# A streaming encoder step: an earlier hand-over of SBUF space at the end of the input projection, and an output projection whose first two tiles run row tile by row tile

## The chip, the cores and the metric

The kernel runs on one core of a Trainium2 chip. The metric is the device time of one execution in microseconds (us). Matmuls run on TensorE (PE); DVE is VectorE, ACT is ScalarE, POOL is GpSimd, and SP is the engine whose queue issues nearly all transfers between HBM and SBUF. "Weight tile" below means 128 output columns of a weight matrix, "row tile" 128 rows of the branch results, all tokens wide.

## The reference, cut to what matters

One layer of an encoder reads 1024 new tokens and 32 tokens of a running stream, 1056 in all, each 1024 wide:

```python
x = layer_norm(x, ln_in_g, ln_in_b)
proj = x @ w_in                                # 17 424 columns
y_a, y_b, y_c, y_d = ...                       # four mixers on columns of proj, each times silu(z)
yb = einsum('blnw,nwd->blnd', ys, w_branch)    # ys stacks the four
gates = sigmoid(col(OFF_G, 4 * D_MODEL) + b_gate)
mixed = einsum('blnd,blnd->bld', gates, yb)
out = mixed @ w_out
x = layer_norm(ALPHA * x + out, ln_g, ln_b)
```

## The kernel before, in words

Activations are kept transposed: 128 channels on the partitions, 1056 tokens along the free axis. For near-float32 accuracy every operand is split into a high part (ACT casts it to fp32r) and a low part (DVE subtracts), and a product is three matmuls: high by high, high by low, low by high. The weight side's split is `wsplit` (L174), the row tiles' is `put_y` (L1323).

The work comes in five stages: the input's normalisation; a first part of the input projection with the mixers A, C and D; the *pairs* (L1012 to L1142); the branch weights (L1343 to L1362); the output projection (L1378 to L1400). The last three are touched.

**Pairs.** The rest of the input projection runs two weight tiles at a time by a fast scheme with seven products in place of eight (L1104 to L1110). It needs sums of halves of the tokens, `TH` and `TL`, for products 2, 3 and 5 (keys 1, 2, 4). They lie in the pool `tt` (L963); the weights' sums and products 5 to 7's operands lie in `w2` (L961). After each product of the last pair `ending(j)` (L1301) runs. After product 5 it closes `tt`, opens the pool `stp` in its place, and starts `stage_y` of the first branch with five row tiles loaded ahead; after product 6 it steps on until two are multiplied.

**Branch weights.** For each branch in the order 0, 3, 2, 1, `stage_y` (L1269) loads for each of eight row tiles a mixer result `t` and its `silu(z)`, both from HBM scratch, and multiplies them (branch 2 has a normalisation and a silu more). `put_y` makes `Y_H` and `Y_L` of them, in the pool `yp`, which takes the place of the input once the pairs are done. Eight jobs, one per weight tile, then multiply them with `w_branch`; each job's eviction multiplies by the gate tile `G` and adds the partial sum `m` of the branches before, which lies in a `padc` tile. The first two jobs run `together` (L230): for each row tile, all three token chunks of both weight tiles, on six PSUM banks. While a branch runs, the next one's row tiles are staged (queue "norm"), and in the last branch `w_out` is loaded and split (L1331).

**Mixing.** The eight `b_mix` generators (L1145) compute mixer B beside all this. The queue "mix" runs them a step at a time, 0.55 steps per turn; a turn comes every few matmuls (`bg`, L169), a step ends at a `yield`. Rate 0 holds the queue during the last pair, and what is left is emptied at once ahead of the third branch (`qm.drain()`, L1371). Convolution tiles and `m` share the two `padc` tiles; `accc` is one tile.

**Output projection.** For token tile 8 (the running stream), then 0 to 7, and for each half of the columns: 24 matmuls over eight row tiles and the three products into one bank, then the residual (L1392) and the layer normalisation. The row tiles are the last branch's `G`.

The tile framework orders each engine's instructions ahead of time by a model of readiness, with the program's order as the priority, and puts in all waits. An instruction that is ready in that model can stand far ahead of its place in the code.

Of the kernel before, what the change touches and what calls it, by code (L numbers as in the profile page):

```python
# [10 lines left out]
F32R = mybir.dt.float32r  # L11
# [42 lines left out]
def encoder_step(ctx: ExitStack, tc: tile.TileContext, I, O):  # L54
# [75 lines left out]
    def ev():  # L130
        return evp.tile([128, T], F32, name="ev")
# [831 lines left out]
    tt = ttc.enter_context(tc.tile_pool(name="tt", bufs=1, side="right"))  # L963
    TH = {j: tt.tile([128, 4, HT], F32R, name=f"th{j}") for j in (1, 2, 4)}
    TL = {j: tt.tile([128, 4, HT], F32R, name=f"tl{j}") for j in (1, 2, 4)}
    lo_t, up_t = slice(0, HT), slice(HT, T)
# [178 lines left out]
    def b_mix(i):  # L1145
# [19 lines left out]
        dve.tensor_sub(xlo, xc, xhi.bitcast(F32))  # L1165
        yield
        g = wk.tile([128, T], F32, name="padc", bufs=2)
        gx = wk.tile([128, T], F32, name="accc", bufs=1)
# [89 lines left out]
    wb = {n: [wb_job(n, d, n != branches[0], n == branches[-1]) for d in range(8)] for n in branches}  # L1258
    stp, first_y = [], []

    def st(dtype=F32, n=T):
        return stp[0].tile([128, n], dtype, name="st", tag="st", bufs=12)

    def sl(dtype=F32, n=T):
        return yp.tile([128, n], dtype, name="sl", tag="sl", bufs=4)

    staged = []

    def stage_y(n, ahead=1):  # L1269

        tz = []

        def load():
            k = len(tz)
            if k < 8:
                tz.append((st(), st()))
                sp.dma_start(tz[k][0], d_t[n][k])
                sp.dma_start(tz[k][1], d_z[n][k])
        if n == 2:
            mu, rs = sl(), sl()  # L1280
            for i, t in enumerate((mu, rs)):
                src = d_mr[9 * i:9 * i + 1, 0:1]
                sp.dma_start(t, bass.AP(tensor=src.tensor, offset=src.offset, ap=[[0, 128], [1, T]]))
        for _ in range(ahead):
            load()
        yield
        yield
        for k, (t, z) in enumerate(tz):
            if n == 2:
                dve.tensor_sub(t, t, mu)  # L1290
                yield
                dve.tensor_mul(t, t, rs)
                act.activation(t, t, AF.Silu, scale=col("c_g", k), bias=col("c_bb", k))
                yield
            dve.tensor_mul(t, t, z)
            load()
            staged.append(t)
            yield
            yield

    def ending(j):  # L1301

        if j == 1:
            qm.rate = 0.0
        if j in (2, 4):
            wb[branches[0]][j // 2 - 1].load()
        if j == 5:
            ttc.close()
            stp.append(ctx.enter_context(tc.tile_pool(name="stp", bufs=1, side="right")))
            first_y.append(stage_y(branches[0], 5))  # L1310
            next(first_y[0])
            next(first_y[0])
        if j == 6:
            while len(staged) < 2:
                next(first_y[0])

# [5 lines left out]

    def put_y(i, y):  # L1323
        Y_H[i] = yp.tile([128, T], F32R, name=f"yh{i}")
        Y_L[i] = yp.tile([128, T], F32R, name=f"yl{i}")
        act.copy(Y_H[i], y)
        dve.tensor_sub(Y_L[i], y, Y_H[i].bitcast(F32))  # L1327

    woh, wol = [], []

    def w_out():  # L1331
        for k in range(KT):
            w = wk.tile([128, T], F32, name="padc", bufs=2)
            o = st if k < 6 else sl
            sp.dma_start(w[:, :D], I["w_out"][k * 128:(k + 1) * 128, :])
            yield
            woh.append(o(F32R, D))
            wol.append(o(F32R, D))
            act.copy(woh[k], w[:, :D])
            dve.tensor_sub(wol[k], w[:, :D], woh[k].bitcast(F32))  # L1340
            yield

    qn = queue("norm", 1.5)  # L1343
    for b, n in enumerate(branches):
        for k in range(8):
            while not staged:
                next(first_y[0])
            put_y(k, staged.pop(0))
        nxt = branches[b + 1] if b + 1 < 4 else None
# [24 lines left out]
    for t, n, i in ((gi, "ln_in", 0), (bi, "ln_in", 1), (go, "ln_out", 0), (bo, "ln_out", 1)):  # L1374
        src = I[n][i:i + 1]
        sp.dma_start(t, bass.AP(tensor=src.tensor, offset=src.offset, ap=[[0, 128], [1, D]]))

    for t in (8, 0, 1, 2, 3, 4, 5, 6, 7):  # L1378
        r = slice(0, 128) if t < 8 else slice(96, 128)
        ts = slice(t * 128, t * 128 + 128) if t < 8 else slice(928, 1056)  # L1380
        xr = wk.tile([128, T], F32, name="padc", bufs=2)[r, :D]
        sp.dma_start(xr, d_x[t, :r.stop - r.start])
        pool.tensor_tensor(xr, xr, gi[r], op=OP.mult)
        pool.tensor_tensor(xr, xr, bi[r], op=OP.add)
        y = ev()
        for c in range(2):
            ps = mmt()
            hs = slice(c * 512, (c + 1) * 512)
            todo = [(a, w, k) for k in range(KT) for a, w in ((Y_H, woh), (Y_L, woh), (Y_H, wol))]
            for n, (a, w, k) in enumerate(todo):  # L1390
                pe.matmul(ps, lhsT=a[k][:, ts], rhs=w[k][:, hs], start=(n == 0), stop=(n == len(todo) - 1))  # L1391
            dve.scalar_tensor_tensor(y[r, hs], xr[:, hs], ALPHA, ps[r], op0=OP.mult, op1=OP.add)  # L1392
# [73 lines left out]
```

## Time and profile before

| | us |
|---|---|
| median of 3 runs | 2256.55 |
| the runs | 2254.4 to 2257.28 |
| the profiled execution | 2259.44 |
| its span, first to last instruction | 2257.7 |
| last pair's last matmul starts | 1747.90 |
| first matmul of the branch weights | 1753.90 |
| first matmul of the output projection | 2144.45 |
| its last matmul starts | 2248.93 |

All positions are counted from the span's start. In the profile, a group or a timeline row names the engine, the line of the code, the operation, and out<-in by the program's tile names: `st<-d_t` is a row tile's load, `yh` and `yl` are Y_H and Y_L, `mm` is a PSUM bank, `accc` and `padc` work tiles. A row of the timeline is: start, duration, then in brackets the idle time before it and what ended that. A row of the waits view is: who waited, for whom, total, number of times, longest. The chain is the work that ended last, followed back step by step.

### The profile page before, as it was taken

What the parts mean: (1) busy time and instruction counts of PE and PEld (TensorE: products, weight loads), DVE (VectorE), ACT (ScalarE), POOL (GpSimd) and SP (SyncE); (2) the same over time, 40 slices, a digit from 0 to 9 for tenths busy, and PEclk for the clock granted to TensorE, in tenths of its full rate; (3) what the DMA queues carried; (4) which work ended last, traced back from release to release, by engine and by line L of the source; (5) the groups of instructions that cost most, each with busy time, mean ns of one, the idle gap of its engine ahead of it and who ended that gap; (6) DMA issues with size and microseconds to landing.
All of it is one profiled execution on the core that took longest, in us unless ns stands there. A gap on an engine that the chain in (4) does not pass through costs nothing.

```text
span 2257.7 us, 38700 instructions
## 1 busy us (share of the span) xinstructions
PE 2198.2 (97%) x15334; PEld 2139.7 (95%) x15334; DVE 1645.8 (73%) x2668; ACT 1006.8 (45%) x1939; POOL 162.0 (7%) x257
## 2 busy tenths in 40 slices
PE   7999999999999999999999999999999999999998
PEld 7999989999999998999999999999999899999976
DVE  7586665599998634778969697966676679855565
ACT  4587876411133443333444444446666245522200
POOL 3121011100000000000000000000000000100043
PEclk9999999999999999999999999999999999999999
DMA  6154454421155564223333333333344898775422
GB/s 233 44 141 126 125 132 108 127 67 48 58 173 177 178 181 135 61 91 99 126 115 114 108 122 127 102 106 121 104 145 137 339 317 309 286 275 173 132 96 75
DMA packets 198160, 323.71 MB, mean 143 GB/s; under 512 B 52793, under 2 KB 117131, under 8 KB 197659
## 3 DMA queue, kind: packets, MB, share of 16 engines
q1 hardware_dynamic: 197979, 321.25, 44.2%
q8 instruction: 120, 1.97, 0.4%
q14 instruction: 61, 0.50, 0.1%
HBM read 211.12 MB, written 110.06 MB: 142 GB/s over the span
## 4 chain that ended last, share of the span: by engine, by line
PE 70%; DVE 9%; DMA 3%; issue 2%; ACT 1%; SPq 0%; DVEq 0%; ACTq 0%
PE mm L1066 31%; PE mm L212 26%; PE mm L1391 4%; PE mm L224 2%; DVE accc L315 2%; DVE bt L564 1%; PE aux L1173 1%; DVE bx L565 1%; DMA Gb<-d_gc 1%; PE aux L679 1%; PE aux L686 1%; DVE yl L1327 1%; PE aux L699 1%; PE aux L698 1%; PE aux L670 1%
## 5 line engine op out<-in xcount | busy, mean ns | idle before, releaser
L315 DVE SCALAR_TENSOR_TENSOR accc<-padc,cols,accc 128x1086 f32<-128x1086 f32 (+2 forms) x250 | 335.1, 1341 | 10.8 <-ACT accc L312 9.4
L212 PE MATMUL mm<-xh,wh 128*128 128x352 f32 (+2 forms) x1600 | 299.4, 325 | 2.7 <-ACT xh L876 0.9
L212 PE MATMUL mm<-xl,wh 128*128 128x352 f32 (+2 forms) x1600 | 301.2, 325 | 0.0
L212 PE MATMUL mm<-xh,wl 128*128 128x352 f32 (+2 forms) x1568 | 295.0, 327 | 3.6 <-DVE wl L181 3.6
L212 PEld LDWEIGHTS mm<-xh,wh 128*128 128x128 f32 x1600 | 259.2, 190 | 5.0 <-DVE padc L737 1.3
L212 PEld LDWEIGHTS mm<-xh,wl 128*128 128x128 f32 x1568 | 257.9, 192 | 5.4 <-DVE wl L181 3.9
L212 PEld LDWEIGHTS mm<-xl,wh 128*128 128x128 f32 x1600 | 259.1, 190 | 1.9 <-issue 0.4
L1066 PE MATMUL mm<-xh,o 128*128 128x264 f32 x1152 | 217.1, 284 | 0.0
L179 ACT CAST wh<-wr 128x1024 fp32r<-128x1024 f32 x96 | 100.7, 1049 | 254.9 <-PE mm L212 212.2
L1066 PEld LDWEIGHTS mm<-xh,o 128*128 128x128 f32 x1152 | 181.3, 188 | 0.0
L1066 PE MATMUL mm<-xl,o 128*128 128x264 f32 x576 | 163.7, 284 | 0.0
L1078 ACT COPY mu<-mm 128x264 f32<-128x264 f32 x216 | 81.0, 377 | 148.2 <-PE mm L1066 146.3
L181 DVE TENSOR_TENSOR wl<-wr,wh 128x1024 fp32r<-128x1024 f32 x96 | 116.8, 1217 | 36.2 <-ACT wh L179 14.7
L1084 DVE TENSOR_TENSOR ev<-mm,mu 128x264 f32<-128x264 f32 x216 | 91.2, 426 | 30.9 <-ACT mu L1078 16.0
L1066 PE MATMUL mm<-xh,wh 128*128 128x264 f32 x576 | 112.3, 285 | 1.1 <-ACT xh L1124 1.1
L1030 ACT CAST o<-wr 128x512 fp32r<-128x512 f32 x108 | 66.8, 619 | 102.4 <-PE mm L1066 86.5
L1066 PE MATMUL mm<-th,o 128*128 128x264 f32 x576 | 112.0, 285 | 0.2
L1066 PE MATMUL mm<-th,wh 128*128 128x264 f32 x576 | 111.8, 285 | 0.0
L1066 PE MATMUL mm<-th,wl 128*128 128x264 f32 x576 | 111.2, 284 | 0.0
L1066 PE MATMUL mm<-xh,wl 128*128 128x264 f32 x576 | 110.6, 284 | 0.0
L1066 PEld LDWEIGHTS mm<-xl,o 128*128 128x128 f32 x576 | 108.2, 188 | 0.0
L212 PE MATMUL mm<-yh,wh 128*128 128x352 f32 x552 | 100.8, 324 | 0.0
(335 smaller groups left out, 4864.9 us busy)
## 6 DMA issues: line engine op xcount, KB each, us to landing
wr<-in_w_in SPq DMA_DIRECT2D x137, 512.0 KB, 3.7
d_z<-ev SPq DMA_DIRECT2D x64, 264.0 KB, 2.2
d_gate<-ev SPq DMA_DIRECT2D x64, 264.0 KB, 2.1
st<-d_t SPq DMA_DIRECT2D x32, 528.0 KB, 6.2
st<-d_z SPq DMA_DIRECT2D x32, 528.0 KB, 8.0
wr<-in_w_branch SPq DMA_DIRECT2D x32, 512.0 KB, 4.4
ev<-d_gate SPq DMA_DIRECT2D x30, 528.0 KB, 5.7
d_mix<-ev SPq DMA_DIRECT2D x24, 528.0 KB, 4.7
```

The source lines that it names most:

```text
L179: act.copy(hi, raw)
L181: dve.tensor_sub(lo, raw, hi.bitcast(F32))
L212: pe.matmul(ps[:, :c[1]], lhsT=w[:, k, :], rhs=r(k)[:, cs(c)], start=(n == 0), stop=(n == len(todo) - 1))
L224: pe.matmul(ps[:, :c[1]], lhsT=w[:, k, :], rhs=r(k)[:, cs(c)], start=(n == 0), stop=(n == len(todo) - 1))
L315: dve.scalar_tensor_tensor(acc, pad[:, i:i + W], col(name, ci, i), acc, op0=OP.mult, op1=OP.add)
L564: dve.tensor_tensor(tv, a[:, j + 1:, j:j + 1].to_broadcast([P, n, m]), x[:, j:j + 1, 0:m].to_broadcast([P, n, m]), op=OP.mult)
L565: dve.tensor_tensor(x[:, j + 1:, 0:m], x[:, j + 1:, 0:m], tv, op=OP.subtract)
L1030: act.copy(t[:, 0:4], src)
L1066: pe.matmul(b, lhsT=w[:, wo + k, :], rhs=XS[name](p, k)[:, sl], start=(start and n == 0), stop=(stop and n == 11), skip_group_check=True)
L1078: act.copy(mu[name][:, c * HC:(c + 1) * HC], b)
L1084: dve.tensor_add(res[i][:, a:a + HC], b, mu[name][:, c * HC:(c + 1) * HC])
L1391: pe.matmul(ps, lhsT=a[k][:, ts], rhs=w[k][:, hs], start=(n == 0), stop=(n == len(todo) - 1))
```

## The change

1. The token sum with key 4 moves from `tt` to `w2`, so `tt` holds two sums and is closed after product 3. `stp` takes its place with 8 tiles in place of 12, and four row tiles of the first branch (`t` and `z`) are loaded at once; two are multiplied after product 5, two after product 6.
2. Row tiles five to eight go into a second set of 8 tiles, `sl` in `yp`, loaded as the first four are put. Their multiplications stand between a tile's cast and its subtraction, one tile ahead.
3. `stage_y` becomes a plain loop, `t` in `st`, `z` in `sl`; `w_out`'s high parts go to `st`, its low parts to `sl`.
4. `b_mix` gets one more `yield` between the split of its convolution and the gate matmuls.
5. The output projection's tiles 8 and 0 run together: for each row tile, three matmuls for each of the four (tile, half) banks. The other seven tiles are as before.

```diff
@@ -961,8 +961,8 @@
     w2 = w2c.enter_context(tc.tile_pool(name="w2", bufs=1))
     ttc = ExitStack()
     tt = ttc.enter_context(tc.tile_pool(name="tt", bufs=1, side="right"))
-    TH = {j: tt.tile([128, 4, HT], F32R, name=f"th{j}") for j in (1, 2, 4)}
-    TL = {j: tt.tile([128, 4, HT], F32R, name=f"tl{j}") for j in (1, 2, 4)}
+    TH = {j: (w2 if j == 4 else tt).tile([128, 4, HT], F32R, name=f"th{j}") for j in (1, 2, 4)}
+    TL = {j: (w2 if j == 4 else tt).tile([128, 4, HT], F32R, name=f"tl{j}") for j in (1, 2, 4)}
     lo_t, up_t = slice(0, HT), slice(HT, T)
 
     def build_t():
@@ -1164,6 +1164,7 @@
         act.copy(xhi, xc)
         dve.tensor_sub(xlo, xc, xhi.bitcast(F32))
         yield
+        yield
         g = wk.tile([128, T], F32, name="padc", bufs=2)
         gx = wk.tile([128, T], F32, name="accc", bufs=1)
         for c in chunks:
@@ -1256,36 +1257,27 @@
 
     branches = (0, 3, 2, 1)
     wb = {n: [wb_job(n, d, n != branches[0], n == branches[-1]) for d in range(8)] for n in branches}
-    stp, first_y = [], []
+    stp = []
 
     def st(dtype=F32, n=T):
-        return stp[0].tile([128, n], dtype, name="st", tag="st", bufs=12)
+        return stp[0].tile([128, n], dtype, name="st", tag="st", bufs=8)
 
     def sl(dtype=F32, n=T):
-        return yp.tile([128, n], dtype, name="sl", tag="sl", bufs=4)
-
-    staged = []
-
-    def stage_y(n, ahead=1):
-
-        tz = []
-
-        def load():
-            k = len(tz)
-            if k < 8:
-                tz.append((st(), st()))
-                sp.dma_start(tz[k][0], d_t[n][k])
-                sp.dma_start(tz[k][1], d_z[n][k])
+        return yp.tile([128, n], dtype, name="sl", tag="sl", bufs=8)
+
+    def stage_y(n, order=None):
+
         if n == 2:
             mu, rs = sl(), sl()
             for i, t in enumerate((mu, rs)):
                 src = d_mr[9 * i:9 * i + 1, 0:1]
                 sp.dma_start(t, bass.AP(tensor=src.tensor, offset=src.offset, ap=[[0, 128], [1, T]]))
-        for _ in range(ahead):
-            load()
-        yield
-        yield
-        for k, (t, z) in enumerate(tz):
+        for k in range(8):
+            t, z = st(), sl()
+            sp.dma_start(t, d_t[n][k])
+            sp.dma_start(z, d_z[n][k])
+            yield
+            yield
             if n == 2:
                 dve.tensor_sub(t, t, mu)
                 yield
@@ -1293,10 +1285,18 @@
                 act.activation(t, t, AF.Silu, scale=col("c_g", k), bias=col("c_bb", k))
                 yield
             dve.tensor_mul(t, t, z)
-            load()
             staged.append(t)
-            yield
-            yield
+
+    staged, first_y = [], []
+
+    def load_first(k, new):
+        first_y.append((new(), new()))
+        sp.dma_start(first_y[k][0], d_t[branches[0]][k])
+        sp.dma_start(first_y[k][1], d_z[branches[0]][k])
+
+    def mul_first(k):
+        t, z = first_y[k]
+        dve.tensor_mul(t, t, z)
 
     def ending(j):
 
@@ -1304,15 +1304,14 @@
             qm.rate = 0.0
         if j in (2, 4):
             wb[branches[0]][j // 2 - 1].load()
-        if j == 5:
+        if j == 3:
             ttc.close()
             stp.append(ctx.enter_context(tc.tile_pool(name="stp", bufs=1, side="right")))
-            first_y.append(stage_y(branches[0], 5))
-            next(first_y[0])
-            next(first_y[0])
-        if j == 6:
-            while len(staged) < 2:
-                next(first_y[0])
+            for k in range(4):
+                load_first(k, st)
+        if j in (5, 6):
+            mul_first(2 * j - 10)
+            mul_first(2 * j - 9)
 
     run_pairs(pairs, ending)
     xstack.close()
@@ -1320,10 +1319,14 @@
     yp = ctx.enter_context(tc.tile_pool(name="yp", bufs=1))
     g2 = yp
 
-    def put_y(i, y):
+    def put_y(i, y, low=True):
         Y_H[i] = yp.tile([128, T], F32R, name=f"yh{i}")
         Y_L[i] = yp.tile([128, T], F32R, name=f"yl{i}")
         act.copy(Y_H[i], y)
+        if low:
+            put_low(i, y)
+
+    def put_low(i, y):
         dve.tensor_sub(Y_L[i], y, Y_H[i].bitcast(F32))
 
     woh, wol = [], []
@@ -1331,11 +1334,10 @@
     def w_out():
         for k in range(KT):
             w = wk.tile([128, T], F32, name="padc", bufs=2)
-            o = st if k < 6 else sl
             sp.dma_start(w[:, :D], I["w_out"][k * 128:(k + 1) * 128, :])
             yield
-            woh.append(o(F32R, D))
-            wol.append(o(F32R, D))
+            woh.append(st(F32R, D))
+            wol.append(sl(F32R, D))
             act.copy(woh[k], w[:, :D])
             dve.tensor_sub(wol[k], w[:, :D], woh[k].bitcast(F32))
             yield
@@ -1343,9 +1345,16 @@
     qn = queue("norm", 1.5)
     for b, n in enumerate(branches):
         for k in range(8):
-            while not staged:
-                next(first_y[0])
-            put_y(k, staged.pop(0))
+            if b == 0:
+
+                if k < 4:
+                    load_first(k + 4, sl)
+                put_y(k, first_y[k][0], False)
+                if 4 <= k + 1 < 8:
+                    mul_first(k + 1)
+                put_low(k, first_y[k][0])
+            else:
+                put_y(k, staged.pop(0))
         nxt = branches[b + 1] if b + 1 < 4 else None
         if nxt == 1:
             qm.drain()
@@ -1375,20 +1384,37 @@
         src = I[n][i:i + 1]
         sp.dma_start(t, bass.AP(tensor=src.tensor, offset=src.offset, ap=[[0, 128], [1, D]]))
 
+    def slices(t):
+        return (slice(0, 128) if t < 8 else slice(96, 128)), (slice(t * 128, t * 128 + 128) if t < 8 else slice(928, 1056))
+
+    def project(ts_):
+
+        pss = {(t, c): mmt() for t in ts_ for c in range(2)}
+        todo = [(a, w, k) for k in range(KT) for a, w in ((Y_H, woh), (Y_L, woh), (Y_H, wol))]
+        for k in range(0, len(todo), 3):
+            for t, c in pss:
+                for n, (a, w, kk) in enumerate(todo[k:k + 3], k):
+                    pe.matmul(pss[t, c], lhsT=a[kk][:, slices(t)[1]], rhs=w[kk][:, c * 512:(c + 1) * 512], start=(n == 0), stop=(n == len(todo) - 1))
+        return pss
+
     for t in (8, 0, 1, 2, 3, 4, 5, 6, 7):
-        r = slice(0, 128) if t < 8 else slice(96, 128)
-        ts = slice(t * 128, t * 128 + 128) if t < 8 else slice(928, 1056)
+        r, ts = slices(t)
         xr = wk.tile([128, T], F32, name="padc", bufs=2)[r, :D]
         sp.dma_start(xr, d_x[t, :r.stop - r.start])
         pool.tensor_tensor(xr, xr, gi[r], op=OP.mult)
         pool.tensor_tensor(xr, xr, bi[r], op=OP.add)
         y = ev()
+        if t == 8:
+            first_ps = project((8, 0))
         for c in range(2):
-            ps = mmt()
             hs = slice(c * 512, (c + 1) * 512)
-            todo = [(a, w, k) for k in range(KT) for a, w in ((Y_H, woh), (Y_L, woh), (Y_H, wol))]
-            for n, (a, w, k) in enumerate(todo):
-                pe.matmul(ps, lhsT=a[k][:, ts], rhs=w[k][:, hs], start=(n == 0), stop=(n == len(todo) - 1))
+            if t in (8, 0):
+                ps = first_ps[t, c]
+            else:
+                ps = mmt()
+                todo = [(a, w, k) for k in range(KT) for a, w in ((Y_H, woh), (Y_L, woh), (Y_H, wol))]
+                for n, (a, w, k) in enumerate(todo):
+                    pe.matmul(ps, lhsT=a[k][:, ts], rhs=w[k][:, hs], start=(n == 0), stop=(n == len(todo) - 1))
             dve.scalar_tensor_tensor(y[r, hs], xr[:, hs], ALPHA, ps[r], op0=OP.mult, op1=OP.add)
         mu, rs = layer_stats(wk, y, r)
         out = O["y_prompt"][ts, :] if t < 8 else O["y_sample"]
```

## The prediction

> **What bounds the kernel now.** First the page: the span, and how full each engine is.
>
> ```profile
> span 2257.7 us, 38700 instructions
> PE 2198.2 (97%) x15334; PEld 2139.7 (95%) x15334; DVE 1645.8 (73%) x2668; ACT 1006.8 (45%) x1939; POOL 162.0 (7%) x257
> ```
>
> TensorE is busy for 97% of the span, so work moved on other engines gives time back only where PE waits or runs at a lowered clock. I read PE's rows of the waits view next, over the three stretches that the diff touches: the pairs' end, the branch weights, the output projection.
>
> ```profile
> PE mm L240 <- ACT yh L1326: 5.7, 1, 5.7
> PE aux L1173 <- ACT ev L1164: 2.5, 2, 2.3
> PE mm L1391 <- ACT yh L1326: 3.1, 1, 3.1
> ```
>
> Each stretch has one long wait: 5.7, 2.3 and 3.1 us. What a wait costs beyond its length is in the windows view (busy time of PE, PEld, DVE, ACT, POOL; granted clock; DMA share; GB/s), here mostly cut where the granted clock changes.
>
> ```profile
> 399.30:402.70 3.40, 1.79 (x12) 1.50 (x11) 0.96 (x2) 3.34 (x11) 0.63 (x1) 1.00 0.84 231
> 402.70:406.10 3.40, 2.45 (x15) 2.17 (x16) 0.90 (x2) 3.11 (x19) 0.00 (x0) 1.00 0.27 77
> 1736.00:1740.00 4.00, 4.00 (x34) 3.80 (x33) 2.11 (x2) 3.67 (x5) 0.00 (x0) 1.00 0.47 145
> 1740.00:1744.00 4.00, 4.00 (x35) 4.00 (x34) 4.00 (x5) 3.33 (x6) 0.00 (x0) 1.00 0.27 68
> 1747.50:1750.90 3.40, 0.68 (x6) 0.47 (x4) 2.03 (x4) 1.47 (x2) 0.00 (x0) 1.00 1.02 409
> 1750.90:1754.30 3.40, 0.40 (x1) 0.40 (x2) 1.68 (x2) 1.07 (x1) 0.00 (x0) 0.51 1.02 414
> 1754.30:1757.70 3.40, 3.40 (x12) 3.19 (x12) 2.26 (x3) 1.07 (x1) 0.00 (x0) 0.50 1.02 413
> 1842.70:1866.00 23.30, 23.30 (x146) 23.30 (x145) 22.05 (x22) 14.40 (x14) 0.00 (x0) 1.00 0.94 319
> 1918.20:1921.60 3.40, 1.12 (x8) 0.82 (x7) 3.40 (x5) 1.07 (x1) 0.00 (x0) 1.00 0.93 332
> 1921.60:1925.00 3.40, 3.40 (x13) 3.40 (x13) 3.32 (x5) 1.28 (x2) 0.00 (x0) 0.50 0.90 292
> 2153.70:2157.10 3.40, 3.40 (x10) 2.61 (x9) 1.47 (x3) 0.00 (x0) 2.00 (x1) 0.50 0.17 70
> ```
>
> The clock is granted in steps of 3.4 us. A step with 1.12 us of PE work is followed by one at 0.50; a step with 1.79 us of work is not. So an idle time of over about 2 us within a step costs another 1.7 us in the next.
>
> **The pairs' end.** The rows, from the timeline, the chain and SP's issues:
>
> ```profile
> 1735.98 0.28 PE L1066 MATMUL mm<-th,wl 128*128 128x264 f32 x1
> 1743.92 0.42 SPq L1277 DMA_DIRECT2D st<-d_t  x1
> 1744.38 6.93 DMA st<-d_z
> 1747.90 0.28 PE L1066 MATMUL mm<-xh,o 128*128 128x264 f32 x1
> 1751.41 1.26 DVE L1295 TENSOR_TENSOR st<-st 128x1056 f32<-128x1056 f32 x1 [1.88 <-DMA st<-d_z]
> 1752.78 1.07 ACT L1326 CAST yh<-st 128x1056 fp32r<-128x1056 f32 x1 [2.48 <-DVE st L1295]
> 1753.88 1.26 DVE L1327 TENSOR_TENSOR yl<-st,yh 128x1056 fp32r<-128x1056 f32 x1 [1.21 <-ACT yh L1326]
> 1755.06 1.25 DVE L1295 TENSOR_TENSOR st<-st 128x1056 f32<-128x1056 f32 x1
> 1782.38 19.12 PE mm L212 x120
> 1808.29 34.48 PE mm L212 x216
> DMA to landing us min/median/max: 6.9/10.1/11.3
> st<-d_t SPq DMA_DIRECT2D x32, 528.0 KB, 6.2
> ```
>
> Now the first row tile is loaded at 1743.92, lands at 1751.3, and is multiplied, cast and subtracted before PE starts. Then each tile passes DVE, ACT, DVE in turn: 3.65 us from one multiplication to the next. PE needs less: 34.48 us for 216 matmuls is 0.1596 us each, so 18 per row tile are 2.87 us. From PE's last matmul of the pairs (1747.90 + 0.12 = 1748.0) to the end of the two weight tiles (1782.4) are 34.4 us, of which 144 x 0.1596 = 23.0 are work.
>
> In the new order the pool is free after the third product, 1735.98 + 0.12 = 1736.1. Eight loads at about 0.45 us of SP each are issued by 1740. They move 8 x 0.54 = 4.3 MB, 10.6 us at 409 GB/s, into a stretch where DMA is at a share of 0.47 and 0.27. They land between 1740 + 6.9 = 1746.9 and 1740 + 11.3 = 1751.3 at the latest; I take 1748, since the queue is empty when they start. SP's later instructions (a weight load and two gate writes) move back by 3.6 us; that weight tile is used at 1782, so it costs nothing. The four multiplications add 4 x 1.26 = 5.0 us to DVE before 1750. DVE has 1.9 us free from 1736 to 1744 and 1.4 from 1747.5 to 1750.9; the rest must displace mixing steps or run up to 1.7 us late. Behind them on DVE wait the last two products' evictions, for whose banks only the second half of a row tile's matmuls waits. PE's twelve Y_H matmuls (1.9 us) cover that.
>
> So after 1748.0: the cast, 1.07 and 0.1 of signalling, PE from 1749.2, then 23.0 us without a gap: 24.2 instead of 34.4, a gain of 10.2. The remaining wait of 1.2 us is below the 1.6 (3.40 - 1.79) that left the clock alone. Row tiles five to eight are loaded from 1748.0 on: at the median landing of 10.1 us the fifth is there at 1758.5 and multiplied at 1759.7, and the fourth tile's subtraction, queued behind it on DVE, ends at 1761.0, against 1749.2 + 3 x 2.87 + 1.9 = 1759.7 when PE wants it: 1.3 late; at 6.9 nothing is late. I take 0.8, nearer to the median. The eighth has until 1769. Forecast: **-9.4**, bounds -10.2 and -4.9 (the second rival).
>
> **The projection.**
>
> ```profile
> 2144.45 0.39 PE L1391 MATMUL mm<-st,yh 128*128 128x512 f32 x1
> 2146.59 0.51 DVE L1248 TENSOR_TENSOR accc<-mm,accc 128x352 f32<-128x352 f32 x1
> 2152.79 0.50 PE L1391 MATMUL mm<-sl,yh 128*128 128x512 f32 x1 [3.08 <-ACT yh L1326]
> 2237.85 0.39 PE L1391 MATMUL mm<-sl,yh 128*128 128x512 f32 x1
> 2243.39 0.39 PE L1391 MATMUL mm<-sl,yh 128*128 128x512 f32 x1
> 2248.93 0.40 PE L1391 MATMUL mm<-sl,yh 128*128 128x512 f32 x1
> ```
>
> Undisturbed, 24 matmuls take 5.54 us, 0.231 each; 431 steps would be 99.5, and 2144.45 to 2248.93 is 104.5. The 5.0 us are the wait for the eighth row tile and the half-clock step after it. New: seven row tiles give 7 x 12 = 84 matmuls, 19.4 us, so the eighth is wanted at 2163.9; it was there at 2152.8. The added wait: four banks at once, where the fourth is freed by the eviction that ends at 2147.1, and PE wants it nine matmuls in, at 2146.5: 0.6 us. The evictions of both first tiles come some 11 us later, beside PE's third tile; the last tile's chain moves with PE. Forecast **-4.4**, bounds -5.0 and -3.1 (the wait alone, the clock falling all the same).
>
> The Trainium skill ("TensorE: Matmul & The Clock Gate", section "Why this matters for your kernels") puts the clock's fall at idle gaps of over some 3 us. The step at 1918.2 with 2.3 us idle contradicts it, and by the rule the first rival would give 1.7 us less.
>
> **The branch weights.** The extra step puts 8 steps more into a queue that advances 0.55 per turn. Rows of the last two mixes:
>
> ```profile
> 1920.18 1.07 ACT L1164 CAST ev<-ev 128x1056 fp32r<-128x1056 f32 x1 [5.12 <-DVE ev L318]
> 1945.64 2.28 DVE L1193 TENSOR_TENSOR_SCAN padc<-accc,ev 128x1024 f32<-128x1024 f32 x1
> 1958.39 0.42 SPq L1148 DMA_DIRECT2D padc<-d_bx  x1
> 1989.86 2.29 DVE L1193 TENSOR_TENSOR_SCAN padc<-accc,ev 128x1024 f32<-128x1024 f32 x1
> ```
>
> The stall at 1918 follows a cast that runs as soon as the convolution (L318) is done, so data set it, not turns. I take **0**: bounds -4.0 (2.3 + 1.7, all of it goes) and +4.0 (a second one like it).
>
> **Without cost.** One token sum in another pool: same bytes, read by the fifth product as before. Staging's z in tiles of their own, w_out split by pool: the same loads and casts; what hides them is PE's queue of matmuls, full at clock 1.00 from 1842.7 to 1866 with DMA at 0.94. Without that cover a late row tile would cost about the 3.65 us of its passage.
>
> **The sum.** 9.4 + 4.4 + 0 = 13.8 us. The profiled execution took 2259.44, 1.7 beyond its span, and would take 2245.6; the median is 2.9 lower: 2256.55 - 13.8 = **2242.8**.
>
> **Rivals.**
> - *The stall at 1918 goes as well*: 4.0 more, 2238.8. For it: the extra step stands exactly between the cast and the matmuls that waited. Against: the reason above.
> - *The early loads come late*: landing 11.3 us after the last issue, the fourth multiplication ends at 1752.6 and the first subtraction, behind it on DVE, at 1753.9, where PE wants it at 1751.1: 2.8 us and 1.7 of clock, 2247.3. For it: those landings stand in the rows. Against: they were measured with DMA full.
> - *The drained mixes hold both padc tiles* (slower). The queue is emptied ahead of the third branch, and by the step count the seventh mix is now almost whole in it. If the third branch's partial sums get no padc tile until both mixes are over, that is 27.7 (1920.18 to 1947.9) + 33.8 (1958.39 to 1992.2) = 61.5 us; the gate tiles last for about four weight tiles, 4 x 72 x 0.1596 = 46.0. PE stalls for 15.5, with three half-clock steps 20.6: 2263.4. It decides once the stall passes 13.8. Against: padc goes to whoever is ready first when one is released.
> - *Changing banks costs clock.* As a mechanism here: every second clock step of the 96 matmuls (22.2 us) at 0.50 makes them 29.6, so 2250.2. Against: the branch weights' bank-by-bank matmuls ran at 1.00 from 1842.7 to 1866. The Trainium skill describes it ("TensorE: Matmul & The Clock Gate", section "A second HAM failure mode: psum-queue depth-cycling"); this case's trace shows no such fall.
> - *The early loads do not start earlier*, the tile framework waiting for more than the two sums: only the projection gains, 2252.2.
>
> **Chances.** Forecast 0.51, stall gone 0.20, late loads 0.13, drained mixes 0.09 (0.05 at full price, 0.04 with one weight tile's 11.5 us, within 0.2%), no earlier start 0.05, clock 0.02. About 0.2%, 4.5 us, is what a measurement of this kernel can tell from no change. Faster: 0.51 + 0.20 + 0.13 + 0.02 = 0.86; same 0.05 + 0.04 = 0.09; slower 0.05. The range runs from all three bounds (10.2 + 5.0 + 4.0, 2237.3) to the clock rival (2250.2).
>
> **What would show it.** Right: eight st loads from about 1736, PE's wait before the first weight tiles near 1.2 us, no half-clock step there, these two tiles in some 25 us; in the projection no wait over 1 us and clock 1.00. Wrong: a multiplication waiting on DMA after 1749, PE waiting on yl, a wait of several us on padc or L1173 between 1860 and 2000 that the old trace has not.

## The result, and the profile after

The changed kernel takes 2268.12 us (median of five runs, 2263.44 to 2272.3) against 2256.06 beside it: 12 us slower, ratio 1.0053 with a 95% interval of 1.0037 to 1.007. The forecast was 2242.8. The profiled execution took 2272.3 us, the slowest of the five.

The page's span and engines, then all of PE's waits from 1000 us on:

```profile
span 2270.6 us, 38698 instructions
PE 2198.8 (97%) x15334; PEld 2142.6 (94%) x15334; DVE 1655.1 (73%) x2668; ACT 1005.6 (44%) x1939; POOL 169.3 (7%) x257
```

```profile
PE aux L1174 <- ACT ev L1164: 7.4, 2, 5.9
PE mm L240 <- DVE yl L1330: 3.5, 1, 3.5
PE mm L1066 <- ACT mu L1078: 2.9, 4, 1.3
PE mm L240 <- ACT yh L1325: 2.5, 1, 2.5
PE aux L1174 <- DVE ev L1165: 2.1, 2, 1.2
PE aux L1174 <- ACT padc L1175: 1.5, 1, 1.5
PE mm L1397 <- DVE accc L1249: 0.4, 1, 0.4
```

PE did the same work (2198.8 us against 2198.2), and the projection's long wait is gone. But PE now waits 11.0 us in all on the mixes' gate matmuls (L1174; L1173 in the code before), 5.9 of it at once, and 3.5 us on a Y_L tile (`yl`) at the pairs' end. The prediction had named both, a new wait of several us on the gates and PE waiting on `yl`, as signs of being wrong. The timeline of ACT, then of PE, at the longest wait (the first row of PE is where the seventh mix's gate matmuls have just ended):

```profile
1983.20 1.28 ACT L312 ACTIVATE accc<-padc,cols 128x1059 f32<-128x1059 f32 x1 [3.87 <-DVE padc L1196]
1989.71 1.07 ACT L1164 CAST ev<-ev 128x1056 fp32r<-128x1056 f32 x1 [4.31 <-DVE ev L318]
```

```profile
1961.60 0.65 PE L224 MATMUL mm<-yh,wh 128*128 128x352 f32 x3
1990.84 0.95 PE L1174 MATMUL aux<-ev,gwh 128*128 128x352 f32 x2 [5.93 <-ACT ev L1164]
```

And the clock around it (windows view, columns as in the prediction), with the one other step at half clock in the branch weights first and that whole stage last:

```profile
1942.09:1945.50 3.41, 3.41 (x14) 3.41 (x13) 1.01 (x3) 2.28 (x3) 0.00 (x0) 0.50 1.02 410
1986.39:1989.81 3.42, 0.00 (x0) 0.00 (x0) 3.26 (x4) 0.10 (x1) 0.00 (x0) 1.00 0.54 165
1989.81:1993.22 3.41, 1.19 (x3) 0.74 (x4) 2.49 (x3) 0.98 (x1) 0.00 (x0) 0.51 1.04 423
1993.22:1996.63 3.41, 1.94 (x6) 1.48 (x7) 3.15 (x7) 2.28 (x3) 0.00 (x0) 0.50 0.89 360
1996.63:2000.05 3.42, 3.42 (x14) 3.42 (x13) 0.00 (x0) 1.53 (x3) 0.00 (x0) 0.50 0.00 0
1786.92:2161.00 374.08, 363.20 (x2235) 361.20 (x2234) 254.92 (x316) 135.89 (x138) 21.22 (x21) 0.98 0.71 248
```

The queue "mix" is emptied ahead of the third branch, so the last mix's gate matmuls stand in PE's queue at a fixed place among the third branch's first matmuls: behind 144 of them, two weight tiles, counted in the trace. PE starts these at 1961.60 and is through at 1990.84 - 5.93 = 1984.9. But the last mix's convolution starts only at 1983.20, when the seventh mix's scan (L1196) has let go of its tiles, and its cast comes at 1989.71. PE stands still, and the next three clock steps run at half.

The last row closes the account of the stage. PE is idle for 374.08 - 363.20 = 10.9 us. In the four steps at half clock it is busy for 3.41 + 1.19 + 1.94 + 3.42 = 10.0 us, which costs half of that, 5.0. The other 358.2 us are work, and by the same working all the kernels below have 357.5 to 358.8 of it: what the stage gains or loses is waits and clock.

Stage by stage, from the rows of the first and last matmul of each stage: "ends" runs from the last pair's last matmul to the last matmul of the first two weight tiles, "branch weights" from there to the stage's last matmul. "7th" is the yield at which the seventh mix stands when the queue is emptied, counted by walking the generators in the program's order (a mix has 18 yields, 19 with the extra one). Each kernel was profiled once; us and ratio are medians against the kernel before on the same chip (2254.07 to 2255.34 in the experiments).

| kernel | us | ratio, 95% | 7th | pairs | ends | branch weights | projection |
|---|---|---|---|---|---|---|---|
| before | 2256.06 | | 18/18 | 753.80 | 34.16 | 362.23 | 104.49 |
| after | 2268.12 | 1.0053 (1.0037, 1.007) | 12/19 | 756.68 | 32.65 | 373.92 | 100.77 |
| after_no_step | 2244.69 | 0.996 (0.9947, 0.9972) | 18/18 | 752.66 | 29.55 | 358.27 | 100.15 |
| before_step | 2259.57 | 1.0023 (1.0014, 1.0032) | 12/19 | 755.66 | 32.08 | 365.15 | 102.03 |
| after_ahead | 2266.61 | 1.0052 (1.0039, 1.0064) | 12/19 | 756.35 | 31.36 | 371.52 | 100.55 |
| before_projection | 2252.59 | 0.999 (0.9979, 1.0) | 18/18 | 754.12 | 33.35 | 359.95 | 100.17 |
| after_step_rate | 2248.99 | 0.9979 (0.9969, 0.9989) | 19/19 | 756.26 | 28.72 | 360.40 | 100.81 |
| after_step_early | 2268.43 | 1.0063 (1.005, 1.0075) | 12/19 | 756.91 | 32.27 | 376.54 | 100.79 |
| after_no_step_lag | 2263.26 | 1.0038 (1.0025, 1.0052) | 12/18 | 754.38 | 30.31 | 373.44 | 100.61 |
| after_no_step_hold | 2254.32 | 1.0002 (0.9993, 1.0011) | 10/18 | 755.72 | 26.12 | 369.10 | 100.74 |
| before_lag | 2265.92 | 1.0046 (1.0028, 1.0065) | 12/18 | 756.19 | 33.89 | 371.66 | 104.47 |
| before_rate | 2262.65 | 1.003 (1.0019, 1.0041) | 18, 8th at 5 | 758.68 | 32.14 | 361.89 | 104.01 |
| after_ends_alone | 2248.18 | 0.997 (0.9958, 0.9981) | 18/18 | 753.05 | 30.61 | 358.35 | 103.91 |
| after_best | 2250.81 | 0.998 (0.9969, 0.9992) | 18/18 | 755.57 | 27.99 | 360.46 | 100.42 |
| after_step_no_projection | 2267.42 | 1.0056 (1.0039, 1.0073) | 12/19 | 756.65 | 32.76 | 376.70 | 102.93 |
| before_step_projection | 2258.04 | 1.0012 (1.0002, 1.0022) | 12/19 | 756.50 | 31.58 | 365.19 | 100.16 |
| after_no_step_545 | 2250.83 | 0.998 (0.997, 0.9989) | 15/18 | 754.08 | 30.50 | 362.61 | 100.68 |
| after_no_step_560 | 2247.44 | 0.9966 (0.9954, 0.9978) | 18, 8th at 5 | 759.62 | 27.65 | 357.32 | 100.49 |

Ahead of the pairs, where nothing is changed, the profiled runs differ by 8 us among themselves (the pairs start at 989.1 to 997.6), so stages are compared, not positions. Four pairs of kernels are the same up to the projection (before and before_projection, after and after_step_no_projection, after_no_step and after_ends_alone, before_step and before_step_projection): in the stages up to there, two profiles of the same code differ by up to 0.8 us in the pairs, 1.1 in the ends and 2.8 in the branch weights.

### The profile page after: what moved, and what is told of

It reads as the page before. It is cut to its first block, busy times and chain, and to the rows that moved or that the text cites. A ratio compares the mean times of both kernels' runs of the same rounds, so it can differ in the third digit from the quotient of the medians.

```text
span 2270.6 us, 38698 instructions
## 1 busy us (share of the span) xinstructions
PE 2198.8 (97%) x15334; PEld 2142.6 (94%) x15334; DVE 1655.1 (73%) x2668; ACT 1005.6 (44%) x1939; POOL 169.3 (7%) x257
## 4 chain that ended last, share of the span: by engine, by line
PE 67%; DVE 10%; DMA 4%; issue 2%; ACT 2%; SPq 0%; DVEq 0%; ACTq 0%
PE mm L1066 30%; PE mm L212 23%; PE mm L1417 3%; DVE accc L315 2%; PE mm L224 2%; DMA st<-d_t 1%; DVE bt L564 1%; PE mm L240 1%; DVE bx L565 1%; PE aux L1174 1%; PE mm L1397 1%; DMA Gb<-d_gc 1%; DVE wl L181 1%; PE aux L679 1%; PE aux L686 1%
```

## The experiments

**Which part is slow.** Undo the extra step, and put it alone into the kernel before; let two row tiles of each later branch be loaded ahead again, as in the kernel before; do the projection alone.

```diff
 after_no_step: after with          before_step: before with
         dve.tensor_sub(xlo, ...)           dve.tensor_sub(xlo, ...)
         yield                              yield
-        yield                     +        yield
 after_ahead: after with
-            t, z = st(), sl()
+            t, z = (sl(), sl()) if k < 2 else (st(), st())
 before_projection: before with project() and first_ps of the change
```

> The changed kernel without the extra step in b_mix. Theory A (the extra step moves the last mixes, so that TensorE's queue reaches their gate matmuls before the split is done): the three stalls at the gate matmuls between 1938 and 1996 and the four of 2.9 us in the pairs go, 10 to 17 us less than the changed kernel: about 2253 (2249 to 2258). Theory B (staging with eight t tiles loads the next branch's row tiles too late, and VectorE waits for them in front of the mixing): the stalls stay, 2264 to 2269.

> The kernel before with the extra step in b_mix alone. Theory A: slower by about what the branch weights and the pairs lost in the changed kernel, 11.7 and 2.9 us: 2266 to 2271, with waits of several us at the gate matmuls near 1980. Theory B: 2252 to 2257, no such waits.

> The changed kernel, extra step kept, with row tiles 0 and 1 of each later branch in the second set of tiles and the others in the first, so that two pairs can again be loaded before the branch before has given its tiles back. Theory A: no change, 2264 to 2270. Theory B: the loads for the second staged branch start before its first Y tile is put, VectorE does not wait for them, and the branch weights take about 362 us again: 2253 to 2258.

> The kernel before with the projection's new order alone. Both theories: the 3.1 us wait and the half-clock step go, 104.5 us become 100.5: 2251.5 to 2253. If the new order cost anything elsewhere: 2256 or more.

Without the step the change is 9.4 us faster than the kernel before, and the waits on the gate matmuls are all but gone. PE's longest wait in after_no_step and its only one on the gates, then the two longest on the gates in before_step:

```profile
PE mm L240 <- ACT yh L1324: 4.3, 1, 4.3
PE aux L1173 <- ACT ev L1164: 0.6, 1, 0.6
```

```profile
PE aux L1174 <- ACT ev L1164: 2.0, 1, 2.0
PE aux L1174 <- ACT padc L1175: 1.6, 1, 1.6
```

The step costs 21 us in the changed kernel (1.0053 less 0.996), more than was expected, and 5 in the kernel before, which lies between the two theories. The theory that staging loads too late fell as the whole cause: after_ahead is as slow as the changed kernel. The projection alone brought 1.5 us (0 to 4.7).

**What the step does: lag or place.** The extra yield makes the eight mixes 160 steps long in place of 152 (18 yields cut a mix into 19 steps), which lags them; and it puts a step's time between the cast and the gate matmuls. Each of the two is tried without the other.

```diff
 after_step_rate: after with        after_no_step_lag: after_no_step with
-    MIX = 0.55                    -    MIX = 0.55
+    MIX = 0.561                   +    MIX = 0.5394
 after_step_early: after with the extra step moved (its yield taken out, and:)
-        for _ in range(4):
+        for _ in range(5):
             yield
```

> The changed kernel with its extra step, but the mix queue advances 0.561 step per turn instead of 0.55, so that at the end of the third branch's turns the recurrence mixes stand as far along (6.6 of 8) as in the kernel before. Theory lag (what costs the 21-23 us is that 160 steps instead of 152 are walked at the old rate, so that the seventh and eighth mix are drained half a mix late and PE's queue meets gate matmuls whose inputs aren't there): the cost goes, 2244 to 2249 us, and PE's longest wait on a gate matmul in 1900-2150 falls from 7.4 us to under 2.5. Rival place (the step between the cast and the gate matmuls puts them into a worse spot of PE's queue wherever the mix stands): 2264 to 2270 us, with a wait of 5 us or more on gate matmuls left.

> The changed kernel with the extra step moved from behind the split of the activations to the loads at the start of each mix: as many steps, the same lag, but the distance from the cast to the gate matmuls is what it was. Theory lag: as slow as the changed kernel, 2260 to 2270 us, with a wait of over 5 us on gate matmuls behind 1970. Rival place: 2243 to 2249 us, as without the step.

> The changed kernel without the extra step, at 0.5394 step per turn instead of 0.55, so that the mixes stand 6.27 of 8 along at the end of the third branch's turns, as they do with the step. Theory lag: the cost comes back without the step, 2260 to 2270 us, with a wait of over 5 us on gate matmuls behind 1970. Rival place: 2243 to 2249 us.

All three went as lag has it: 2248.99 with the step but no lag, 2268.43 and 2263.26 with the lag elsewhere or without the step. The longest of PE's waits on the gates in 1850 to 2150, of after_step_rate, after_step_early and after_no_step_lag:

```profile
PE aux L1174 <- ACT ev L1164: 1.2, 2, 0.9
```

```profile
PE aux L1173 <- ACT ev L1164: 8.7, 2, 6.2
```

```profile
PE aux L1173 <- DVE ev L1165: 7.2, 1, 7.2
PE aux L1173 <- ACT ev L1164: 3.1, 1, 3.1
```

So it is the count of steps against the fixed rate. What the yield's place costs is little: after_step_rate is 4.3 us above after_no_step (0.9979 less 0.996), and their intervals just meet.

PE's rows say why a lag of six steps or more hurts. In all the kernels that have it the last mix's gates stand behind the same 144 matmuls of the third branch, and only 136 to 216 matmuls lie between the seventh mix's gates and them, 22 to 34 us at 0.16 us each (144 and 23.3 us in the changed kernel). The rest of the seventh mix and the last mix's convolution and cast have to fit into that; in the changed kernel they took 29.2 us, from 1961.60 to 1990.84. In after_no_step 251 matmuls lie between, 40 us.

**The pairs' end.** Hold the mixing back earlier, so that DVE is free there.

```diff
 after_no_step_hold: after_no_step with
-    MIX = 0.55
+    MIX = 0.558
...
                     next(st["nxt"], None)
+                    if j == 4 and n == len(pairs) - 2:
+                        qm.rate = 0.0
...
-            qm.rate = MIX
+            qm.rate = 0.55
```

> The changed kernel without the extra step, mixing held from the fourth product of the last pair but one instead of from the first of the last, at 0.558 step per turn until then (the same number of steps by the end of the pairs) and 0.55 behind. Theory: at the pairs' end VectorE ran 4.00 of 4.00 us from 1739 to 1751 because mixing issued earlier was still in its queue, and that held the last evictions, the sigmoid and the casts behind it. With it gone, the last product's eviction follows its matmul within 0.6 us, PE's wait for the first split row tile falls from 4.3 to 2-3 us, the half-clock step behind it goes, and the stretch from the last pair's matmul to the end of the first two token sums is 25 to 27 us instead of 29.6: 2240 to 2243 us. Rival: the wait is the chain of eviction, sigmoid and cast by itself: still 4 us or more, 29 us, and 2244 to 2246 us.

The stage went as expected, 26.12 us in place of 29.55; the time did not, since the queue had lost more turns than the higher rate gave back (step 10 of 18), and PE waited 5.2 us on a gate matmul from 1967.7 on. A version with rates of 0.565 before the hold and 0.59 behind it, otherwise the same, and the change without the step and the projection:

> The changed kernel without the extra step, mixing held from the fourth product of the last pair but one, at 0.565 step per turn before and 0.59 behind, so that the seventh mix stands at step 18 of 18 at the third branch as in the kernel before (with 0.558 and 0.55 it stood at step 10). Theory: the pairs' end of the held kernel (26.1 us from the last pair's matmul to the end of the first two sums, against 29.6) without its 5.2 us wait on gate matmuls: 2244.7 - 3.4 = 2241.3 us, 2238 to 2243. Rival: the faster mixing behind the pairs costs PE waits of its own in the first two branches: 2244 to 2250.

> The changed kernel without the extra step and with the projection as before: the pairs' end and the staging alone. If the parts add up: 2244.7 + 1.5 = 2246.2 us (2244 to 2249), so that the pairs' end and the staging bring 8 us of the 9.4. If the projection is worth the 4.4 of the forecast here: 2249 or more, and pairs' end and staging 5 us.

after_best has no lag and no wait over 2.3 us, and is still slower than after_no_step: its pairs took 755.57 us in place of 752.66, its branch weights 360.46 in place of 358.27. The rival (faster mixing costs waits of its own) is nearer. By its median after_no_step stays the fastest kernel of the study. after_ends_alone says that the pairs' end and the staging bring 7 us.

**A slope or a valley, and why 21 against 5.** Other rates, on both kernels, and the step with each half of the change. The edits are the lines above: MIX = 0.5394 and 0.56 in the kernel before; 0.545 and 0.56 in after_no_step; the step with the projection as before; the step and the new projection in the kernel before.

> The kernel before at 0.5394 step per turn instead of 0.55: at the third branch the seventh mix stands at step 12 of 18, as with the extra step in the changed kernel. Open is why the step cost 5.5 us in the kernel before and 21 to 24 in the changed one. Theory staging: in the kernel before, VectorE has multiplied two row tiles of the fourth branch before the third branch's splits, so fewer stand ahead of the seventh mix's chain, and the lag costs little: 2257 to 2262 us. Rival threshold: the kernel before with the step only just escaped, and a lag of the same size costs it as much as the changed kernel: 2268 to 2276 us.

> The kernel before at 0.56 step per turn: five steps further at the third branch than at 0.55. Theory: at 0.55 the kernel before has just enough lead (its gate matmuls wait 1.5 us in all in 1900-2150), so more of it brings 0 to 2 us: 2251.5 to 2254.5 us. Rival: the mixes' lead bounds it still, and 4 us or more are won, which would then not be the change's in any later kernel with a higher rate: under 2250.

> The changed kernel without the step at 0.545 step per turn: the seventh mix at step 15 of 18 at the third branch, between 18 at 0.55 (2244.7 us) and 12 at 0.5394 (2263.3). Theory slope (each step of lag costs about 3 us): 2251 to 2257 us. Theory cliff (nothing until PE's queue overtakes the mix, then all): 2243 to 2247 or 2260 to 2266.

> The changed kernel without the step at 0.56 step per turn: five steps further at the third branch than at 0.55. Theory slope or cliff in the lag alone: more lead costs nothing, 2241 to 2246 us. Theory valley (the mixes' place against PE's queue is fitted to 0.55, as before_rate's 7 us say): 2249 to 2256 us, most of it from longer pairs and waits of PE on the copies of the products there.

> The changed kernel with its extra step, but the projection as before. If the step's larger cost comes from the pairs' end and the staging: 2267 to 2272 us (the changed kernel plus the 2 to 3 us that the projection was worth). If the projection's order takes part: 2253 to 2259 us.

> The kernel before with the extra step and the new projection order, pairs' end and staging as before. If the step's larger cost comes from the pairs' end and the staging: 2255 to 2260 us. If from the projection's order: 2264 or more.

A lag of 3 steps costs the changed kernel 4.5 us (0.998 less 0.996), of 6 steps 17.6; both its steepness and before_lag's 10 us lie between the theories. A lead of 5 steps costs it 1.4 us, which its intervals don't tell from nothing, and the kernel before 6.8. Where the lead costs is the pairs, 759.62 us against 752.66. PE's waits of after_no_step_560, then its timeline at the longest of them (DVE, ACT, PE):

```profile
PE mm L1066 <- ACT mu L1078: 3.4, 3, 2.6
```

```profile
1689.73 0.69 DVE L1034 TENSOR_TENSOR s<-wr 128x512 f32<-128x512 f32 x1 [2.91 <-DMA wr<-in_w_in]
```

```profile
1690.51 0.62 ACT L1030 CAST wh<-s 128x512 fp32r<-128x512 f32 x1 [5.06 <-DVE s L1034]
1691.03 0.65 ACT L1078 COPY mu<-mm 128x264 f32<-128x264 f32 x2
```

```profile
1691.46 0.39 PE L1066 MATMUL mm<-xh,wl 128*128 128x264 f32 x1 [2.65 <-ACT mu L1078]
```

ACT was idle for 5.06 us with a cast of the next pair's weight sums next in its queue, waiting for DVE and, through it, for a load. The copy of a product that PE had finished by 1688.9 ran only behind that cast, and PE, which goes on in the same bank, waited 2.65 us. The changed kernel has four waits on these copies (2.9 us in all), the kernel before and after_no_step none. The four kernels at 0.55 with 18 steps have one between them (0.7 us, before_projection); each of the others has 1.1 to 3.9 us. So 0.55 with 18 steps is a place where these orders fit, and moving the mixes either way costs.

The step interacts with the pairs' end and the staging, not with the projection: it costs 19 us with them (1.0056 less 0.997) and 5 without (1.0012 less 0.999). Which of the two is not settled, but the trace shows one way. DVE's timeline of before_step, then of after, from the end of the seventh mix's gates to its scan:

```profile
1955.78 1.25 DVE L1177 TENSOR_TENSOR ev<-ev,accc 128x1056 f32<-128x1056 f32 x1
1958.42 2.42 DVE L1296 TENSOR_TENSOR st<-st 128x1056 f32<-128x1056 f32 x2
1967.15 2.29 DVE L1194 TENSOR_TENSOR_SCAN padc<-accc,ev 128x1024 f32<-128x1024 f32 x1
```

```profile
1966.71 1.26 DVE L1177 TENSOR_TENSOR ev<-ev,accc 128x1056 f32<-128x1056 f32 x1
1969.35 3.60 DVE L1287 TENSOR_TENSOR st<-st,sl 128x1056 f32<-128x1056 f32 x3
1974.02 1.26 DVE L1287 TENSOR_TENSOR st<-st,sl 128x1056 f32<-128x1056 f32 x1
1978.11 1.26 DVE L1287 TENSOR_TENSOR st<-st,sl 128x1056 f32<-128x1056 f32 x1
1980.65 2.29 DVE L1194 TENSOR_TENSOR_SCAN padc<-accc,ev 128x1024 f32<-128x1024 f32 x1
```

Five products of the next branch stand in the changed kernel's chain where two stood: with only eight `st` tiles none of them can be loaded before this branch's are released. That makes 13.9 us from L1177 to the scan against 11.4. In after_ahead two products go ahead as in the kernel before. PE's rows of before_step at the last mix's gates, then of after_ahead at the seventh's and the last's:

```profile
1976.33 0.59 PE L1174 MATMUL aux<-ev,gwh 128*128 128x352 f32 x2 [1.96 <-ACT ev L1164]
```

```profile
1940.54 0.43 PE L1174 MATMUL aux<-ev,gwh 128*128 128x352 f32 x1 [3.27 <-ACT ev L1164]
1987.23 0.58 PE L1174 MATMUL aux<-ev,gwh 128*128 128x352 f32 x2 [1.96 <-ACT ev L1164]
```

So the bunched products are what makes the last mix's wait 5.9 us in place of 2.0. But what after_ahead won there it lost at the seventh's gates, 3.3 us against 1.4 in the changed kernel, and its times are no better. Nor is the staging needed for a loss: before_lag, with neither the step nor the new staging, has branch weights of 371.66. Why the kernel before bears the step and not the lag stays open.

## Why the prediction was wrong, point by point

**The branch weights: the step that failed.** "The stall at 1918 follows a cast that runs as soon as the convolution (L318) is done, so data set it, not turns. I take 0", with bounds of 4 us either way. The profiled stage grew by 11.7 us, and by 15.7 against after_no_step, nearly all of it 10.3 us more of waits and 5.0 of half clock. The reading of that stall was not the question. The 8 added steps were counted, and their effect looked for at the one wait that the trace already had; it fell on the emptied queue, where the seventh mix now stood at step 12 of 19 and the eighth could not start before it ended. The rival of the drained mixes had the right place, and by the step count it named the right cause, the seventh mix still in the queue. It had the wrong wait (no padc tile for the partial sums, no wait of PE in the trace after goes back to one) and too small a chance, 0.09. The rival in which the extra step takes the stall at 1918 away fell as well: in the changed kernel that wait, on the seventh mix's gates, is the smaller of the two in the first row of waits above (1.4 us of the 7.4), and without the step it is 0.6. In the kernel before the step did take it away (0.2 us in before_step), and the stage grew all the same. The 4.0 us were no steady price either: in before_projection, the same code up to there, the stall is 0.8 us with no half-clock step.

The sum had no term for the pairs, which grew by 2.9 us in the profile: the waits on the products' copies, which come with moved mixes.

**The pairs' end: right in kind, half in size.** The loads start after the third product and are there in time. after_no_step's SP (the first and the last of the eight issues), DVE and ACT:

```profile
1732.21 0.33 SPq L1293 DMA_DIRECT2D st<-d_t  x1
1735.74 0.46 SPq L1294 DMA_DIRECT2D st<-d_z  x1
```

```profile
1743.40 1.31 DVE L315 SCALAR_TENSOR_TENSOR accc<-padc,cols,accc 128x1059 f32<-128x1059 f32 x1
1746.13 0.42 DVE L1084 TENSOR_TENSOR ev<-mm,mu 128x264 f32<-128x264 f32 x1
```

```profile
1746.59 0.73 ACT L1092 ACTIVATE ev<-ev,cols 128x528 f32<-128x528 f32 x1 [2.34 <-DVE ev L1084]
1747.23 3.98 ACT L1324 CAST yh<-st 128x1056 fp32r<-128x1056 f32 x4
```

The gain is 34.16 - 29.55 = 4.6 us without the step, 1.5 with it, for a forecast of 9.4. The step that failed: for the late evictions' banks "only the second half of a row tile's matmuls waits". The banks were not what hurt. The last eviction (1746.13) feeds the last sigmoid (1746.59), and the four casts stand behind that sigmoid on ACT, so PE started at 1748.34, 4.3 us after its last matmul, and not 1.2. The mixing that DVE was to displace was not displaced: DVE was busy without a gap from 1739 to 1749. With it held back, the same chain, DVE then ACT:

```profile
1746.89 0.43 DVE L1084 TENSOR_TENSOR ev<-mm,mu 128x264 f32<-128x264 f32 x1
```

```profile
1747.36 0.74 ACT L1092 ACTIVATE ev<-ev,cols 128x528 f32<-128x528 f32 x1 [2.17 <-DVE ev L1084]
1748.00 3.99 ACT L1326 CAST yh<-st 128x1056 fp32r<-128x1056 f32 x4
```

There PE waits 2.3 us and the stage is 8.0 us shorter than before. So DVE's mixing was 3.4 us of what was missing (29.55 - 26.12), and the eviction and the sigmoid ahead of the cast the rest. With the step it went worse: PE waited 2.5 us for the cast and then 3.5 for the first Y_L, because a scan of the fourth mix (2.29 us) and the fourth product stood on DVE ahead of the subtractions. Six Y_H matmuls stand on PE ahead of the first Y_L there, not the twelve that were to cover it. The rival of late loads fell: none of the first four products waited for a transfer. So did that of no earlier start: the loads go out 11.6 us ahead of the pairs' last matmul, where the kernel before had 4.0.

**The projection: right.** Forecast -4.4; the profiled stage went from 104.49 to 100.77, and to 100.15 without the step. The bank wait was 0.4 us for a forecast of 0.6. The stage in the windows view, but for its ends:

```profile
2158.20:2260.00 101.80, 101.38 (x443) 82.35 (x442) 73.30 (x117) 4.85 (x11) 45.60 (x18) 1.00 0.25 89
```

The clock stayed at 1.00 though the banks change every three matmuls, so the rival of changing banks fell. The fall that the Trainium skill describes for a cycling PSUM queue ("TensorE: Matmul & The Clock Gate", section "A second HAM failure mode: psum-queue depth-cycling") shows in none of the twelve profiled projections with the new order. By times the gain is smaller, 1.5 us alone and 2.3 beside the rest (0.997 less 0.996), the first with an interval that reaches 4.7: the old order lost a half-clock step in the profiles of some kernels and not of others (below).

**Without cost: only with the lead.** In after_ends_alone the new staging costs nothing that shows: its branch weights take 358.35 us. With the lag it bunches DVE's products ahead of the seventh mix's scan, and the last mix's wait grows from 2.0 to 5.9 us. Whether the staging or the pairs' end makes up the rest of the step's 19 us against 5 is open.

**The sum without the step.** after_no_step took 2244.69 us, close to the forecast, but not by its terms: in the profiles the pairs' end gave 4.6 us in place of 9.4, and the branch weights, taken at 0, gave 4.0, where two profiles of the same code differ by up to 2.8. That is luck more than a right sum.

## What to carry to other kernels

Where a queue of background steps is walked at a fixed rate, adding a step to a generator moves everything behind it: count where each generator stands when the queue is emptied or held, before and after, and count how much of PE's work lies between that place and the matmuls that need its result. A rate that was tuned is a place as much as a speed, so whoever adds a step sets the rate with it (0.561 took back 17 of the 21 us here: 1.0053 less 0.9979) and tries both sides. When a cast is to run "as soon as its data are there", look at what stands ahead of it in its engine's queue.

## What was not expected of the hardware

One and the same wait, 2.2 us in the old projection, cost half a clock step in one kernel and nothing in another. The windows of before_rate, then of before_step, cut where the clock is granted:

```profile
2151.00:2154.40 3.40, 1.18 (x5) 0.66 (x4) 2.21 (x2) 1.07 (x1) 1.53 (x1) 1.00 0.16 39
2154.40:2157.80 3.40, 3.40 (x9) 2.62 (x9) 0.96 (x1) 0.00 (x0) 1.51 (x1) 0.50 0.31 117
```

```profile
2149.00:2152.40 3.40, 1.87 (x9) 1.18 (x7) 2.85 (x3) 0.43 (x1) 2.40 (x1) 1.00 0.19 61
2152.40:2155.80 3.40, 2.71 (x12) 2.20 (x13) 1.72 (x2) 0.64 (x1) 0.41 (x1) 1.00 0.44 154
```

In the first the wait lies within one step, which leaves 1.18 us of work; in the second it straddles two, 1.87 and 2.71, and the clock stays. The stages were 104.01 and 102.03 us. Of the six profiled kernels with the old order four lost such a step (before, before_lag, before_rate, after_ends_alone) and two did not (before_step, and after_step_no_projection with a wait of 2.5 us). So a profiled loss of this kind need not be the kernel's, and the prediction took the 5.0 us of one profile for it; that it also comes and goes between executions of one kernel is likely by these rows, but not shown. The Trainium skill says that the window is free-running ("TensorE: Matmul & The Clock Gate", section "What's actually happening"), with which these rows agree.

A step that is already at half clock needs more work to be followed by a full one. In the steps at 2154.40 in before_rate and at 1996.63 in the changed kernel PE worked throughout, and full clock came next. In the changed kernel's step at 1993.22 it worked for 1.94 us and the next was at half again, though after a step at full clock 1.87 us were enough (before_step, 2149.00). So the prediction's rule of some 2 us of idle time holds for a step at full clock alone.
